# A hybrid recurrent layer step: the samples' state passes in one row, the residual's norm tile by tile in the second feed-forward product, and a third buffer of split weights from the merges on

## The chip, the cores and the metric

The kernel runs on one core of a Trainium2 chip. The metric is the time of one execution on the device in microseconds (us), the median of several runs. Engines go by short names: PE is TensorE, which multiplies matrices (PEld is its weight load), DVE is VectorE, ACT is ScalarE, POOL is GpSimd, and SP is SyncE, from whose queue most transfers are issued.

## What is computed

One inference step of a decoder layer, for a prompt of 512 tokens and for 8 samples of 4 tokens each, which share all weights. The width is 1024, the feed-forward width 4096. Cut to what matters:

```
proj = x @ w_in + b_in
h_gla = head_rmsnorm(gated_linear_scan(q, k, v, g, s_gla)) * silu(gr)     # GLA, 4 heads, dv 96
h_ml  = head_layernorm(mlstm_scan(q, k, v, i, f, c, n, m)) * sigmoid(mo)  # mLSTM
h_hg  = head_rmsnorm(gated_linear_scan(qh, kh, vh, log_f, s_hg)) * silu(hgt)  # HGRN2, 4 heads, dv 64
gates = sigmoid(mg)
merged = gates[0] * (h_gla @ w_up_gla) + gates[1] * (h_ml @ w_up_ml) + gates[2] * (h_hg @ w_up_hg)
x = layernorm(alpha * x + merged @ w_out, ln1_g, ln1_b)
hid = square(relu(x @ w_ff_up))
x = layernorm(alpha * x + hid @ w_ff_down, ln2_g, ln2_b)
```

In a gated linear scan each token's state is S_t = diag(exp g_t) S_{t-1} + k_t^T v_t, its output q_t S_t. The prompt starts from zero states, each sample from its own, and all final states are outputs too.

## The kernel before

**Layout and products.** The prompt's 512 columns and the samples' 32 stand side by side: T = 544 columns, worked on as two halves of 272 (HT). Activations lie with features on the 128 partitions. A product is computed on float32r operands of which each is split into a high part and the rest (names ending in h and l), as three products: high x high, high x low, low x high. `wload` (L133) does this for 1024 or fewer weight columns: a transfer from SP's queue into `raw` (three buffers), a copy by ScalarE into `wh` (L141), and VectorE's `raw - wh` into `wl` (L142). `wh` and `wl` have two buffers each, those of the pool `wp`. `mm` (L145) issues the matmuls, all on line L158: for each of the weights' 128-row blocks 3 x 2 matmuls of 272 columns. `gemm` (L163) is a load with its product, into one of two PSUM tiles named `g`, so that one is evacuated while the other is filled. `xgemm` (L172) is such a product with the layer's input `xh`, `xl`.

**Stages, in the order of the program.** First projections; the mLSTM; GLA's projections; GLA's scan by `gated` (L351); the merge of the mLSTM branch; HGRN2's projections; HGRN2's scan by `gated` again; the merge of the GLA branch; that of the HGRN2 branch; the output product with the first layer norm (`ln_tile`, `ln_end`); the feed-forward part in two blocks of 2048; the second layer norm, whose last products are shared with it.

**The scan.** `gated` takes the prompt in two units of 256 columns and the samples as a third. `levels` (L357) builds a unit's attention, level by level: a decay by VectorE and ScalarE, products with it on VectorE (`ke`, `qe`), four matmuls on TensorE (`lv`, L410) and a masked copy out. `chunk` (L461) then applies it and carries the state on. `sample` (L494) reads the samples' old states: for each of the two head pairs p the states come by a transfer on ScalarE's queue into `Ss`, and eight matmuls, one for each sample n, multiply `Ss` with that sample's queries `qx` (L509). Such a matmul has few columns, and the program writes it as one with two blocks of four; on the chip it is two matmuls. I call it a pass. Its weights have 96 columns in GLA and 64 in HGRN2, where those of other matmuls have 128. After a pair's passes the update of its states follows: `kvs` (L517) on TensorE, and a multiply and add on VectorE. `finish_rows` (L282) transposes normalised outputs (`oT`, L286) and multiplies them into the branch's gate.

**Merges.** `Merge` (L851) has three kinds of steps: `gates` (a product of 48 matmuls with the input, evacuated and put through a sigmoid), `split` (the branch's output into `hh`, `hl`), and `products` (the branch's product of 12 or 18 matmuls, multiplied by its gate and added to `merged`). The first two merges do four gates and then four products, twice over. The last one (`mr_`, L945) alternates: gate m + 1, product m.

**The residual.** After the output product `x1` (the memory of `merged`) holds the centred sum that the first layer norm takes. The feed-forward product uses a form of it that isn't normalised, and puts the norm in behind it (L1037 to L1039, with `ne` the negative mean and `rstd` the inverse deviation). The normalised `x1` itself is only wanted as the residual, in the second feed-forward product of the first block (L1062). Its three steps, an add of `ne` (L1052), a multiplication by `rstd` (L1054) and ScalarE's scale and bias (L1055), stand in the loop of the 16 tiles of the first feed-forward product of block 0: an add behind each even tile, the other two behind each odd one.

**What sets the order.** A scheduler puts the program's instructions in order for each engine by priority, which is at first the order in which they are written. `tc.high_priority(OFF)` puts a step as early as its operands allow; a negative argument puts it later. The passes have such a one, of 380 and 4 more for each sample:

```
with tc.high_priority(-(BEHIND + 4 * n)):
    nc.tensor.matmul(
        oT[0:dv, p * 64:(p + 1) * 64].rearrange("p (a b) -> p a b", a=2)[:, :, 4 * n:4 * n + 4],
        Ss[:, n, 0:dv], qx[:, p, n], start=False, stop=(p == 1 and n == 7))
```

Each engine then runs its queue in that order, and waits by semaphores for the others.

Of the kernel before, what the change touches and what calls it, by code (L numbers as in the profile page):

```python
# [6 lines left out]
F32 = mybir.dt.float32  # L7
F32R = mybir.dt.float32r
BF16 = mybir.dt.bfloat16
I32 = mybir.dt.int32  # L10
AF = mybir.ActivationFunctionType
ALU = mybir.AluOpType
PSUM = bass.MemoryType.PSUM

T = 544
# [6 lines left out]
ALPHA = 2.0 ** 0.25  # L22
# [2 lines left out]
NEG = -1e30  # L25
XMIN = -44.0
OFF = 1000000
BEHIND = 380
NF = 4
NWARM = 10  # L30
ADDP, MULP, AFFD = (), (), ()
# [4 lines left out]
V_L1G, V_L1B, V_L2G, V_L2B, V_QS, NV = 76, 84, 92, 100, 108, 109  # L36
# [7 lines left out]
def build(tc, I, O):  # L44
    nc = tc.nc
    with ExitStack() as ctx:
        const = ctx.enter_context(tc.tile_pool(name="const", bufs=1))
        wp = ctx.enter_context(tc.tile_pool(name="wp", bufs=2))
# [20 lines left out]
        for k in range(KD):  # L69
# [11 lines left out]
            for i, n in (sorted(terms) if k == KD - 1 else terms):  # L81
                w, a = ((fh, xh), (fl, xh), (fh, xl))[n]
                for hf in range(2):
                    nc.tensor.matmul(first_ps[i][hf], w[:, i * 128:(i + 1) * 128], a[:, k, hf * HT:(hf + 1) * HT],  # L84
                                     start=(k == 0 and n == 0), stop=(k == KD - 1 and n == 2))
# [43 lines left out]
        def vcol(c):  # L129
            return vec[:, c:c + 1]  # L130


        def wload(src, nk):  # L133

            n = nk * 128
            raw = wp.tile([128, 1024], F32, tag="raw", name="raw", bufs=3)
            nc.sync.dma_start(out=raw[:, 0:n], in_=src)
            h = wp.tile([128, 1024], F32R, tag="wh", name="wh")
            l = wp.tile([128, 1024], F32R, tag="wl", name="wl")
            with tc.high_priority(OFF):  # L140
                nc.scalar.activation(out=h[:, 0:n], in_=raw[:, 0:n], func=AF.Copy)  # L141
                nc.vector.tensor_tensor(out=l[:, 0:n], in0=raw[:, 0:n], in1=h[:, 0:n].bitcast(F32), op=ALU.subtract)  # L142
            return h, l
# [19 lines left out]
        def gemm(srcs, ah, al, ext=0):  # L163
            units = []
            for src, n in srcs:
                h, l = wload(src, n)
                units.append((h, l, n))
            ps = psg.tile([128, 2, 512], F32, tag="g", name="g")
            mm(ps, units, ah, al, ext)
            return ps if ext else ps[:, :, 0:HT]  # L170
# [4 lines left out]
        def halves(ap):  # L175
            return ap.rearrange("p (a b) -> p a b", a=2)
# [5 lines left out]
        def pool(name, bufs=1, side=None):  # L182
            st = ExitStack()
            return st, st.enter_context(tc.tile_pool(name=name, bufs=bufs, side=side, reuse_waits="tile"))
# [166 lines left out]
        def gated(q, k, b, sc, dv, vtok, sname, nt, gate):  # L351
# [142 lines left out]
            def sample():  # L494
                at, P, qx, k3 = (st[2][n] for n in ("at", "P", "qx", "k3"))
                oT = psr.tile([128, 512], F32, tag="r", name="oTs")
                for h in range(4):
                    nc.tensor.matmul(oT[0:dv, h * 32:(h + 1) * 32], vtok[0:32, 4, h * dv:(h + 1) * dv], at[0:32, h, 0:32],
                                     start=(h == 0), stop=False)
                v3 = stack_v(vtok[0:32, 4, 0:d4], d4)  # L500
                nb = 512 // dv // 4 * 4
                yield
                for p in range(2):
                    Ss = t1.tile([128, 8, 97], F32, tag="Ss", name="Ss")
                    nc.scalar.dma_start(out=Ss[:, :, 0:dv], in_=I[sname][p])
                    for n in range(8):

                        with tc.high_priority(-(BEHIND + 4 * n)):
                            nc.tensor.matmul(  # L509
                                oT[0:dv, p * 64:(p + 1) * 64].rearrange("p (a b) -> p a b", a=2)[:, :, 4 * n:4 * n + 4],  # L510
                                Ss[:, n, 0:dv], qx[:, p, n], start=False, stop=(p == 1 and n == 7))
                    yield
                    vxs = [spread_v(v3[:, (2 * p + e) * dv:(2 * p + e + 1) * dv], dv, True) for e in range(2)]
                    for n0 in range(0, 8, nb):
                        kvs = psr.tile([128, 512], F32, tag="r", name="kvs")
                        for e in range(2):
                            nc.tensor.matmul(kvs[:, 0:nb * dv], k3[:, p, e, :], vxs[e][:, n0 * dv:(n0 + nb) * dv], start=(e == 0), stop=(e == 1))  # L517
                        for n in range(n0, n0 + nb):
                            nc.vector.scalar_tensor_tensor(
                                Ss[:, n, 0:dv], Ss[:, n, 0:dv], P[:, p, 4 * n + 3:4 * n + 4],  # L520
                                kvs[:, (n - n0) * dv:(n - n0 + 1) * dv], ALU.mult, ALU.add)
                    nc.scalar.dma_start(out=O[sname + "_s"][p], in_=Ss[:, :, 0:dv])
                    yield
                oTs = t1.tile([97, 128], F32, tag="oTs", name="oTsb", bufs=1)
                nc.scalar.activation(out=oTs[0:dv], in_=oT[0:dv, 0:128], func=AF.Copy)
                o = psr.tile([128, 512], F32, tag="r", name="osm")
                for h in range(4):
                    nc.tensor.transpose(o[0:32, h * dv:(h + 1) * dv], oTs[0:dv, h * 32:(h + 1) * 32], ident[0:dv, 0:dv])
                on = rms_rows(32, o[0:32, 0:d4].rearrange("p (a b) -> p a b", a=4), dv)
                yield  # L530
                finish_rows(32, on, nt, gate, TP)
# [48 lines left out]
        for j in range(3):  # L580
            if M_X + j < NF:
                ps = first_ps[M_X + j]
            else:
                ps = xgemm(M_X + j)
                ps = [ps[:, 0, :], ps[:, 1, :]]
# [11 lines left out]
        for j in range(3):  # L597
            y = tile2([128, PADN], "cvy")
            ys.append(y)
            y = y[:, 0:NCV]  # L600
# [208 lines left out]

        pipe([ml_chunk(c) for c in (0, 4, 1, 2, 3)])  # L810
        mls.close()


        def open_kq():
# [22 lines left out]
        for j in range(2):  # L837
            ps = xgemm(M_K + j)
# [48 lines left out]
        hls, hlp = pool("hl")  # L887
        mgs, mgp = pool("mg")
        merged = mgp.tile([128, KD, T], F32, name="merged")
        mm_ = Merge(1, mgate, 3, "wup_ml", first=True)  # L890
        mm_.gates(0, gbp)
        mm_.split()
# [10 lines left out]
        for j in range(2):  # L903
# [5 lines left out]
            l = ftile("hl_")  # L909
# [118 lines left out]
        for blk in range(2):  # L1028
            hid = []
            deep = [hl3("hdh", "hh"), hl3("hdl", "hl")] + [w6.tile([128, 3 * T], F32R, tag="w6", name="hdw").rearrange("p (a b) -> p a b", a=3) for i in range(2)]  # L1030
            for m in range(16):
                ps = gemm([(I["wff1"][blk * 16 + m], KD)], lambda k: x1h[:, k, :], lambda k: x1l[:, k, :], ext=2)

                gw = fp.tile([128, 2], F32, tag="gw", name="gw", bufs=3)
                nc.scalar.activation(out=gw, in_=ps[:, 1, HT:HT + 2], func=AF.Copy)
                r_ = fp.tile([128, T], F32, tag="relu", name="relu", bufs=2)
                nc.vector.scalar_tensor_tensor(halves(r_), halves(ne), gw[:, 0:1], ps[:, :, 0:HT], ALU.mult, ALU.add)  # L1037
                nc.vector.tensor_tensor(out=r_, in0=r_, in1=rstd, op=ALU.mult)  # L1038
                nc.scalar.activation(out=r_, in_=r_, func=AF.Relu, bias=gw[:, 1:2])  # L1039
                nc.scalar.activation(out=r_, in_=r_, func=AF.Square)  # L1040
                if m < 6:
                    h, l = deep[m // 3][:, m % 3, :], deep[2 + m // 3][:, m % 3, :]
                else:
                    h = fp.tile([128, T], F32R, tag=f"hidh{m}", name="hidh")
                    l = fp.tile([128, T], F32R, tag=f"hidl{m}", name="hidl")
                split(h, l, r_)
                hid.append((h, l))
                if blk == 0:

                    y = x1[:, m // 2, :]  # L1050
                    if m % 2 == 0:
                        nc.vector.tensor_tensor(out=y, in0=y, in1=ne, op=ALU.add)  # L1052
                    else:
                        nc.vector.tensor_tensor(out=y, in0=y, in1=rstd, op=ALU.mult)  # L1054
                        nc.scalar.activation(out=y, in_=y, func=AF.Identity, scale=vcol(V_L1G + m // 2), bias=vcol(V_L1B + m // 2))  # L1055
            hh_, hl_ = (lambda k: hid[k][0]), (lambda k: hid[k][1])
            for m in range(KD if blk == 0 else KD - 2):
                w = I["wff2"][blk, m]
                ps = gemm([(w[:, 0:1024], 8), (w[:, 1024:2048], 8)], hh_, hl_)
                xm = halves(x1[:, m, :])  # L1060
                if blk == 0:
                    nc.vector.scalar_tensor_tensor(xm, xm, ALPHA, ps, ALU.mult, ALU.add)  # L1062
                else:
                    nc.vector.tensor_tensor(out=xm, in0=xm, in1=ps, op=ALU.add)
                    ln_tile(x1, m, slice(0, T), None)
# [49 lines left out]
        sts.close()  # L1115
        mgs.close()
        hls.close()
        gbs.close()


# [115 lines left out]
```

## Time and profile before

| | |
|---|---|
| Time, median of 3 runs | 937.22 us (937.22, 938.57, 936.66) |
| The profiled execution | 937.23 us, its span 935.1 us |
| TensorE's granted clock, mean | 0.995 |
| TensorE busy | 915.1 us, 98% |
| VectorE busy | 570.4 us, 61% |
| ScalarE busy | 436.9 us, 47% |
| GpSimd busy | 46.8 us, 5% |
| Bytes moved | 82.73 MB, mean 88 GB/s |

A row of the trace's timeline has the start in us from the span's start, the time from there to the end of the row's last instruction, engine, line, operation, what it writes and reads, the sizes and how many instructions the row joins; in brackets stand the idle time of the engine just before and what ended it. Matmuls are pipelined: the end of one is modelled and lies behind the start of the next, so times on TensorE are best taken from start to start. A row of the waits has the waiting engine and what it waited for, then the total in us, how many times, and the longest. The chain that ended last is followed back from the last instruction, at each step to what released it.

### The profile page before, as it was taken

Reading aid. Unit: us, or ns where it says so; the run is one execution under the profiler, and the core shown is the slowest. Engines: PE = TensorE matmul, PEld = TensorE weight load, DVE = VectorE, ACT = ScalarE, POOL = GpSimd, SP = SyncE. Lnnn points to the kernel's source line nnn. Section 1 sums busy time; section 2 is a strip of 40 time slices with the busy share of each in tenths; the row PEclk is TensorE's granted clock in tenths of the full one; section 3 lists DMA queues with packets and bytes.
Section 4 is the critical chain, followed back from the end, with each engine's and each line's share of the span. In section 5 each row is a group of like instructions: output and inputs, shape, how many; then the busy total and the mean of one; then the engine's idle time right before and its main releaser. Section 6 shows DMA issues by size and latency. Waiting matters only on the chain.

```text
span 935.1 us, 17425 instructions
## 1 busy us (share of the span) xinstructions
PE 915.1 (98%) x7271; PEld 897.1 (96%) x7271; DVE 570.4 (61%) x995; ACT 436.9 (47%) x822; POOL 46.8 (5%) x62
## 2 busy tenths in 40 slices
PE   9999999999999999999999989999999999999995
PEld 7998999999999989999999989999999999999994
DVE  5886468867877658785558695553222455545345
ACT  5395222975536755535444375542111355432215
POOL 1302130001001001000000000000000000000000
PEclk9999999999999999999999999999999999999998
DMA  7321232123122113023235222222222222322302
GB/s 265 122 71 66 72 114 73 37 82 100 63 93 94 54 29 119 27 79 107 68 118 149 99 71 88 91 91 90 91 86 79 86 91 91 91 90 81 100 23 96
DMA packets 37598, 82.73 MB, mean 88 GB/s; under 512 B 12708, under 2 KB 18340, under 8 KB 37520
## 3 DMA queue, kind: packets, MB, share of 16 engines
q1 hardware_dynamic: 25072, 73.28, 24.1%
q10 hardware_dynamic: 12384, 8.33, 3.1%
q8 instruction: 57, 0.93, 0.4%
q14 instruction: 21, 0.17, 0.1%
q0 software_dynamic: 64, 0.02, 0.0%
HBM read 76.51 MB, written 5.09 MB: 87 GB/s over the span
## 4 chain that ended last, share of the span: by engine, by line
PE 93%; DVE 4%; ACT 2%; DMA 1%; issue 1%; ACTq 0%; DVEq 0%
PE g L158 79%; PE lv L410 3%; PE g L84 3%; DVE wl L142 1%; PE o L467 1%; PE qkp L682 1%; PE oTs L509 1%; ACT wh L141 1%; PE oTm L770 1%; DVE merged L1054 1%; PE oT L286 0%; PE vt L259 0%; PE o L470 0%; DMA fw<-in_wfirst 0%; DVE merged L1052 0%
## 5 line engine op out<-in xcount | busy, mean ns | idle before, releaser
L141 ACT ACTIVATE wh<-raw 128x1024 fp32r<-128x1024 f32 (+2 forms) x139 | 133.3, 959 | 231.9 <-PE g L158 199.4
L142 DVE TENSOR_TENSOR wl<-raw,wh 128x1024 fp32r<-128x1024 f32 (+2 forms) x139 | 155.2, 1117 | 134.9 <-ACT wh L141 133.1
L158 PE MATMUL g<-xh,wl 128*128 128x272 f32 x752 | 161.9, 293 | 1.2 <-DVE wl L142 1.2
L158 PE MATMUL g<-xh,wh 128*128 128x272 f32 x752 | 161.0, 293 | 0.3 <-DVE z L833 0.3
L158 PE MATMUL g<-xl,wh 128*128 128x272 f32 x752 | 160.8, 292 | 0.0
L158 PEld LDWEIGHTS g<-xh,wl 128*128 128x128 f32 x752 | 119.4, 189 | 2.9 <-DVE wl L142 2.5
L158 PEld LDWEIGHTS g<-xh,wh 128*128 128x128 f32 x752 | 119.6, 189 | 1.5 <-DVE z L833 0.5
L158 PEld LDWEIGHTS g<-xl,wh 128*128 128x128 f32 x752 | 119.4, 189 | 1.0 <-issue 0.5
L158 PE MATMUL g<-x1h,wh 128*128 128x272 f32 (+1 forms) x512 | 106.5, 289 | 2.8 <-DVE relu L1037 2.8
L158 PE MATMUL g<-x1l,wh 128*128 128x272 f32 (+1 forms) x512 | 106.5, 289 | 0.0
L158 PE MATMUL g<-x1h,wl 128*128 128x272 f32 (+1 forms) x512 | 106.3, 289 | 0.0
L158 PEld LDWEIGHTS g<-x1h,wh 128*128 128x128 f32 x512 | 80.9, 189 | 3.3 <-DVE relu L1037 3.2
L158 PEld LDWEIGHTS g<-x1l,wh 128*128 128x128 f32 x512 | 81.2, 189 | 0.1
L158 PEld LDWEIGHTS g<-x1h,wl 128*128 128x128 f32 x512 | 80.9, 189 | 0.0
L1039 ACT ACTIVATE relu<-relu,gw 128x544 f32<-128x544 f32 x32 | 24.0, 750 | 73.8 <-DVE relu L1038 73.8
L158 PE MATMUL g<-hidh,wh 128*128 128x272 f32 x280 | 58.1, 288 | 0.0
L158 PE MATMUL g<-hidl,wh 128*128 128x272 f32 x280 | 58.1, 289 | 0.0
L158 PE MATMUL g<-hidh,wl 128*128 128x272 f32 x280 | 57.9, 288 | 0.0
L158 PEld LDWEIGHTS g<-hidh,wl 128*128 128x128 f32 x280 | 43.9, 188 | 0.1
L158 PEld LDWEIGHTS g<-hidl,wh 128*128 128x128 f32 x280 | 43.9, 188 | 0.0
L158 PEld LDWEIGHTS g<-hidh,wh 128*128 128x128 f32 x280 | 43.8, 188 | 0.0
L215 DVE TENSOR_SCALAR gb<-g,vec 128x544 f32<-128x544 f32 x24 | 18.8, 783 | 31.5 <-PE g L158 31.3
(398 smaller groups left out, 1661.0 us busy)
## 6 DMA issues: line engine op xcount, KB each, us to landing
raw<-in_wff SPq DMA_DIRECT2D x64, 512.0 KB, 3.5
raw<-in_win SPq DMA_DIRECT2D x47, 512.0 KB, 3.2
xr<-in_xT SPq DMA_DIRECT2D x16, 272.0 KB, 3.4
raw<-in_wout SPq DMA_DIRECT2D x8, 512.0 KB, 3.7
out_yT<-merged SPq DMA_DIRECT2D x8, 272.0 KB, 2.2
fw<-in_wfirst ACTq DMA_DIRECT2D x8, 256.0 KB, 5.4
raw<-in_wup_ml SPq DMA_DIRECT2D x8, 192.0 KB, 2.3
raw<-in_wup_gla SPq DMA_DIRECT2D x8, 192.0 KB, 2.3
```

What stands on the lines that cost most here:

```text
L84: nc.tensor.matmul(first_ps[i][hf], w[:, i * 128:(i + 1) * 128], a[:, k, hf * HT:(hf + 1) * HT], start=(k == 0 and n == 0), stop=(k == KD ...
L141: nc.scalar.activation(out=h[:, 0:n], in_=raw[:, 0:n], func=AF.Copy)
L142: nc.vector.tensor_tensor(out=l[:, 0:n], in0=raw[:, 0:n], in1=h[:, 0:n].bitcast(F32), op=ALU.subtract)
L158: nc.tensor.matmul(ps[:, hf, 0:w_], w, a(k)[:, hf * HT:hf * HT + w_], start=(k == 0 and s == 0), stop=(k == nk - 1 and s == 2))
L215: nc.vector.tensor_scalar(out, ps, vcol(col), XMIN, ALU.add, ALU.max)
L410: nc.tensor.matmul(lv[0:R, o:o + 2 * H].rearrange("p (a b) -> p a b", a=2), Kv[:, p, c * R:(c + 1) * R], Q[:, p, :, c * H:(c + 1) * H], st ...
L467: nc.tensor.matmul(o[:, h * dv:(h + 1) * dv], at[:, c * 4 + h, :], vtok[:, cc, h * dv:(h + 1) * dv], start=(h == 0), stop=(cc == 0 and h = ...
L509: nc.tensor.matmul(oT[0:dv, p * 64:(p + 1) * 64].rearrange("p (a b) -> p a b", a=2)[:, :, 4 * n:4 * n + 4], Ss[:, n, 0:dv], qx[:, p, n], s ...
L682: nc.tensor.matmul(ps[0:96, hf, 0:HT], w[:, i, h, :], a[h][:, hf * HT:(hf + 1) * HT], start=(n == 0), stop=(n == 2))
L770: nc.tensor.matmul(oT[0:97, h * 32 + 4 * n:h * 32 + 4 * n + 4], Cs[:, n, :], qF[h][:, 4 * n:4 * n + 4], start=False, stop=(h == 3 and n == 7))
L1039: nc.scalar.activation(out=r_, in_=r_, func=AF.Relu, bias=gw[:, 1:2])
L1054: nc.vector.tensor_tensor(out=y, in0=y, in1=rstd, op=ALU.mult)
```

## The change

**Passes.** The negative priority around L509 is gone, with its constant. The passes have the priority of the place where they are written.

**Residual.** The three steps are taken out of the loop of the first feed-forward product. In the loop of the second one, in block 0, they are written ahead of each tile's product, for that tile alone, and write a new tile `xn` (one buffer). `x1` keeps the centred sum until the evacuation, which now reads `xn`.

**Buffers.** A new pool `w3` is opened after the mLSTM's memory is closed, with one `wh` and one `wl` (8 KB of each partition). From the first merge on, every third call of `wload` takes its two tiles from it, and the others from `wp` as before.

```diff
--- before.py
+++ after.py
...
-BEHIND = 380
...
+        more_w, nload = [], [0]
+
         def wload(src, nk):
...
-            h = wp.tile([128, 1024], F32R, tag="wh", name="wh")
-            l = wp.tile([128, 1024], F32R, tag="wl", name="wl")
+            w_ = more_w[0] if more_w and nload[0] % 3 == 2 else wp
+            nload[0] += 1
+            h = w_.tile([128, 1024], F32R, tag="wh", name="wh")
+            l = w_.tile([128, 1024], F32R, tag="wl", name="wl")
...
                     for n in range(8):
-
-                        with tc.high_priority(-(BEHIND + 4 * n)):
-                            nc.tensor.matmul(
-                                oT[0:dv, p * 64:(p + 1) * 64].rearrange("p (a b) -> p a b", a=2)[:, :, 4 * n:4 * n + 4],
-                                Ss[:, n, 0:dv], qx[:, p, n], start=False, stop=(p == 1 and n == 7))
+                        nc.tensor.matmul(
+                            oT[0:dv, p * 64:(p + 1) * 64].rearrange("p (a b) -> p a b", a=2)[:, :, 4 * n:4 * n + 4],
+                            Ss[:, n, 0:dv], qx[:, p, n], start=False, stop=(p == 1 and n == 7))
...
         mls.close()
+        w3s, w3p = pool("w3")
...
         merged = mgp.tile([128, KD, T], F32, name="merged")
+        more_w.append(w3p)
         mm_ = Merge(1, mgate, 3, "wup_ml", first=True)
...
                 hid.append((h, l))
-                if blk == 0:
-
-                    y = x1[:, m // 2, :]
-                    if m % 2 == 0:
-                        nc.vector.tensor_tensor(out=y, in0=y, in1=ne, op=ALU.add)
-                    else:
-                        nc.vector.tensor_tensor(out=y, in0=y, in1=rstd, op=ALU.mult)
-                        nc.scalar.activation(out=y, in_=y, func=AF.Identity, scale=vcol(V_L1G + m // 2), bias=vcol(V_L1B + m // 2))
             hh_, hl_ = (lambda k: hid[k][0]), (lambda k: hid[k][1])
             for m in range(KD if blk == 0 else KD - 2):
                 w = I["wff2"][blk, m]
+                if blk == 0:
+
+                    xn = fp.tile([128, T], F32, tag="xn", name="xn", bufs=1)
+                    nc.vector.tensor_tensor(out=xn, in0=x1[:, m, :], in1=ne, op=ALU.add)
+                    nc.vector.tensor_tensor(out=xn, in0=xn, in1=rstd, op=ALU.mult)
+                    nc.scalar.activation(out=xn, in_=xn, func=AF.Identity, scale=vcol(V_L1G + m), bias=vcol(V_L1B + m))
...
                 if blk == 0:
-                    nc.vector.scalar_tensor_tensor(xm, xm, ALPHA, ps, ALU.mult, ALU.add)
+                    nc.vector.scalar_tensor_tensor(xm, halves(xn), ALPHA, ps, ALU.mult, ALU.add)
...
         hls.close()
+        w3s.close()
```

Three places show what the scheduler makes of it. A row has the line, the operation, what it writes and reads, the size and how many such instructions follow one another; the line numbers of after are 3 to 6 higher. The first place is TensorE in the HGRN2 samples: `oTs` from `qx` and `Ss` is a pass, `lv` a level of the prompt's first unit, `kvs` the states' update, `g` from `xh` or `xl` a gate product of the merge that follows. Before:

```order
L410 MATMUL lv<-qe_3863,ke_3861 128x128 x4
L509 MATMUL oTs<-qx,Ss 64x2x4 x2
L410 MATMUL lv<-qe_3862,ke_3860 128x128 x4
L158 MATMUL g<-xh,wl 128x272 x2
L509 MATMUL oTs<-qx,Ss 64x2x4
L158 MATMUL g<-xh,wh 128x272 x2
L158 MATMUL g<-xl,wh 128x272 x2
L509 MATMUL oTs<-qx,Ss 64x2x4
L158 MATMUL g<-xh,wl 128x272 x2
L517 MATMUL kvs<-vx,k_3915 128x512
L158 MATMUL g<-xh,wh 128x272 x2
L509 MATMUL oTs<-qx,Ss 64x2x4
```

And after:

```order
L413 MATMUL lv<-qe_3866,ke_3864 128x128 x4
L510 MATMUL oTs<-qx,Ss 64x2x4 x8
L413 MATMUL lv<-qe_3865,ke_3863 128x128 x4
L510 MATMUL oTs<-qx,Ss 64x2x4 x2
L518 MATMUL kvs<-vx,k_3918 128x512
L510 MATMUL oTs<-qx,Ss 64x2x4 x6
L161 MATMUL g<-xh,wl 128x272 x2
```

Before, the 16 passes stand in 15 rows among the products, one of them of two passes; after, in rows of 8, 2 and 6, and the products follow. In GLA the 16 passes stood in one row of nine and seven lone ones, and stand in rows of 11 and 5.

The second place is VectorE where the first feed-forward product begins: `rstd<-m,rstd` belongs to the end of the first layer norm, `wl` is a weight split, `relu<-ne,gw,g` is the evacuation of a tile. Before:

```order
L996 TENSOR_TENSOR rstd<-m_6319,rstd 128x272
L1052 TENSOR_TENSOR merged<-merged,ne 128x544 x8
L142 TENSOR_TENSOR wl<-raw,wh 128x1024
L1037 SCALAR_TENSOR_TENSOR relu<-ne,gw,g 128x544
L1054 TENSOR_TENSOR merged<-merged,rstd 128x544 x8
L142 TENSOR_TENSOR wl<-raw,wh 128x1024
L1037 SCALAR_TENSOR_TENSOR relu<-ne,gw,g 128x544
```

And after:

```order
L1000 TENSOR_TENSOR rstd<-m_6322,rstd 128x272
L1058 TENSOR_TENSOR xn<-merged,ne 128x544
L145 TENSOR_TENSOR wl<-raw,wh 128x1024
L1041 SCALAR_TENSOR_TENSOR relu<-ne,gw,g 128x544
L1059 TENSOR_TENSOR xn<-xn,rstd 128x544
L1042 TENSOR_TENSOR relu<-relu,rstd 128x544
L145 TENSOR_TENSOR wl<-raw,wh 128x1024
L1041 SCALAR_TENSOR_TENSOR relu<-ne,gw,g 128x544
```

Eight adds and eight multiplications stood in rows there; one of each is left, and the other seven stand in the second feed-forward product, one ahead of each product's evacuation.

The third place is TensorE where the last merge begins: `oT` are the last transposes of the HGRN2 scan, whose outputs are multiplied by the gate and split into `hh` and `hl`, and `g` from `hh` is the first product with them. Before:

```order
L286 MATMUL oT<-ident,on 128x128 x2
L158 MATMUL g<-xl,wh 128x272
L158 MATMUL g<-xh,wl 128x272 x2
L158 MATMUL g<-xh,wh 128x272 x2
L158 MATMUL g<-xl,wh 128x272 x2
L158 MATMUL g<-xh,wl 128x272 x2
L158 MATMUL g<-xh,wh 128x272 x2
L158 MATMUL g<-xl,wh 128x272 x2
L158 MATMUL g<-xh,wl 128x272 x2
L158 MATMUL g<-hh,wh 128x272 x2
```

And after:

```order
L289 MATMUL oT<-ident,on 128x128 x2
L161 MATMUL g<-xh,wh 128x272
L161 MATMUL g<-xl,wh 128x272 x2
L161 MATMUL g<-xh,wl 128x272 x2
L161 MATMUL g<-hh,wh 128x272 x2
```

15 products stood between the two, and five do now. Another place of the same kind lies behind the GLA samples: between the last level of the prompt's first unit (`lv` from `kg`) and the level before it stood 73 products, and stand 95 now.

More of the change, by code (lines that the diff above doesn't have):

```diff
@@ L811, in build @@
         mls.close()
+        w3s, w3p = pool("w3")
+        pass
         def open_kq():
```

## The prediction

> **What bounds the kernel now.** I read the page's first part and the chain that ended last, then the waits, then the timeline at the places that both name. From the page:
>
> ```profile
> span 935.1 us, 17425 instructions
> ## 1 busy us (share of the span) xinstructions
> PE 915.1 (98%) x7271; PEld 897.1 (96%) x7271; DVE 570.4 (61%) x995; ACT 436.9 (47%) x822; POOL 46.8 (5%) x62
> ```
>
> And the longest piece of the chain (start, us, what):
>
> ```profile
> 551.50 288.96 PE g L158 x2293
> ```
>
> TensorE is busy 98% of the span, and for 289 us on end the chain is nothing but products: 2293 in 288.96 us, 0.126 us each, with no wait between. Something can be won only where matmuls start further apart than that. TensorE's waits name such places (us in total, times, longest):
>
> ```profile
> PE g L158 <- DVE relu L1037: 2.8, 2, 2.2
> PE g L158 <- DVE wl L142: 1.9, 7, 0.7
> ...
> PE lv L410 <- DVE qe L402: 0.7, 1, 0.7
> ```
>
> The wait for relu lies ahead of the first feed-forward product, that for wl in the last merge, that for qe behind the GLA samples: the change touches all three. An idle time counts from where a matmul's end is modelled, which is later than the next start could have been. So I measure a gap from start to start: next start, minus start of the last pair, minus two matmuls (0.25 us).
>
> **The residual's norm.** VectorE at the start of the first feed-forward product:
>
> ```profile
> 537.53 5.17 DVE L1052 TENSOR_TENSOR merged<-merged,ne 128x544 f32<-128x544 f32 x8 [0.16 <-ACT ne L997]
> 542.62 1.22 DVE L142 TENSOR_TENSOR wl<-raw,wh 128x1024 fp32r<-128x1024 f32 x1
> 543.76 0.78 DVE L1037 SCALAR_TENSOR_TENSOR relu<-ne,gw,g 128x544 f32<-128x544 f32 x1
> 544.45 5.17 DVE L1054 TENSOR_TENSOR merged<-merged,rstd 128x544 f32<-128x544 f32 x8
> ```
>
> TensorE at the same time, around the two gaps:
>
> ```profile
> 541.94 0.41 PE L158 MATMUL g<-x1h,wl 128*128 128x272 f32 x2
> 544.59 0.53 PE L158 MATMUL g<-x1h,wh 128*128 128x272 f32 x2 [2.24 <-DVE relu L1037]
> ...
> 550.51 0.41 PE L158 MATMUL g<-x1h,wl 128*128 128x272 f32 x2
> 551.50 0.52 PE L158 MATMUL g<-x1h,wh 128*128 128x272 f32 x2 [0.57 <-DVE relu L1037]
> ```
>
> Eight adds stand ahead of the first evacuation (L1037), eight multiplications ahead of the second, 5.17 us each, while both PSUM tiles of the products are full. TensorE stands for 544.59 - 541.94 - 0.25 = 2.40 us and for 551.50 - 550.51 - 0.25 = 0.74 us, 3.1 us together. With the change one add (5.17 / 8 = 0.65) is left ahead of the first and one multiplication ahead of the second. From 537.53 the queue is 0.65 + 1.22 + 0.78, so the first tile is free at about 540.2 (541 if the split wl must wait a little for wh), and TensorE asks for it at 542.19: at least 1 us to spare. **Term: -3.1 us**; by the row of waits it is -2.8, and 0 if the evacuation is late for another reason.
>
> The other seven tiles' steps go to the second feed-forward product. There VectorE waits for each product's end (first row), and the affine step that ScalarE has to do took 5.97 / 8 = 0.75 us (second row):
>
> ```profile
> DVE merged L1062 <- PE g L158: 31.5, 8, 4.0
> ...
> 545.20 5.97 ACT L1055 ACTIVATE merged<-merged,vec 128x544 f32<-128x544 f32 x8 [1.95 <-DVE merged L1054]
> ```
>
> A product there is 96 matmuls, 12.1 us, and in each VectorE idles 31.5 / 8 = 3.9 us before the evacuation. Into that fit the 0.65 + 0.65 us that it gets more, and 0.75 us on ScalarE. L1064 now waits for the affine step too; behind it in VectorE's queue stand the next tile's add and a split, and TensorE waits for neither within a product, since the other PSUM tile takes 12.1 us to fill. **Term: 0.** Without both covers it would be 7 x (0.65 + 0.65 + 0.75) = 14.4 us.
>
> **The third buffer.** In the last merge a gate product (48 matmuls) and a branch product (12) alternate. TensorE in one such turn and at the first output product:
>
> ```profile
> 461.62 0.41 PE L158 MATMUL g<-xl,wh 128*128 128x272 f32 x2
> 462.20 0.52 PE L158 MATMUL g<-xh,wl 128*128 128x272 f32 x2 [0.16 <-DVE wl L142]
> ...
> 479.05 0.41 PE L158 MATMUL g<-ml,wh 128*128 128x272 f32 x2
> 480.17 0.52 PE L158 MATMUL g<-mh,wl 128*128 128x272 f32 x2 [0.71 <-DVE wl L142]
> ```
>
> The two halves of the split that this turn waits for, on ScalarE and on VectorE:
>
> ```profile
> 459.82 1.06 ACT L141 ACTIVATE wh<-raw 128x1024 fp32r<-128x1024 f32 x1 [3.35 <-PE g L158]
> ...
> 460.92 1.23 DVE L142 TENSOR_TENSOR wl<-raw,wh 128x1024 fp32r<-128x1024 f32 x1
> ```
>
> The split of the next gate's weights takes 1.06 + 1.23 = 2.3 us and starts only when the gate before it has released its buffer; the 12 matmuls of the branch and the first four of the gate, 16 x 0.126 = 2.0 us, do not cover it. The gap is 462.20 - 461.62 - 0.25 = 0.33 us, at the output product 0.87 us. The row of waits counts seven; with the other five like the first that is 6 x 0.33 + 0.87 = 2.85 us. With three buffers a gate's weights go where the branch product before the last gate had its own, and that is free a whole gate, 6 us, earlier. **Term: -2.9 us**, from -1.9 (the idle time as the row of waits has it) to -3.4, since TensorE's idle time ahead of all products in the seven turns came to that:
>
> ```profile
> PEld g L158: 3.4, 7
> ```
>
> That row is the weight loads' idle time (us, times), which begins when the load before has ended. VectorE at 61% and ScalarE at 47% of the span have room for splits that come earlier. The feed-forward products, in the chain's long piece, wait for no split now, and gain nothing.
>
> **The passes.** In the HGRN2 samples a pass (L509) is two matmuls with 64 weight columns among products with 128. TensorE there:
>
> ```profile
> 328.16 0.40 PE L509 MATMUL oTs<-qx,Ss 128*64 128x8 f32 x4
> 328.49 1.16 PE L410 MATMUL lv<-qe,ke 128*128 128x128 f32 x8
> ...
> 330.05 0.52 PE L158 MATMUL g<-xh,wh 128*128 128x272 f32 x2
> 330.40 0.41 PE L158 MATMUL g<-xl,wh 128*128 128x272 f32 x2
> 330.74 0.28 PE L509 MATMUL oTs<-qx,Ss 128*64 128x8 f32 x2
> 330.95 0.52 PE L158 MATMUL g<-xh,wl 128*128 128x272 f32 x2
> ```
>
> From 330.05 to 330.95 run four products (0.50) and one pass: a lone pass costs 0.40 us. From its first start to the next instruction's, a lone pass takes 330.95 - 330.74 = 0.21 us and a row of two 328.49 - 328.16 = 0.33: the second one added 0.12. So each pass that joins a row saves 0.28 us. The order had 15 rows for these 16 passes and has three now (8, 2 and 6): 12 x 0.28 = 3.4 us. In the GLA samples, with 96 columns, two lone passes four products apart:
>
> ```profile
> 185.60 0.26 PE L509 MATMUL oTs<-qx,Ss 128*96 128x8 f32 x2
> ...
> 186.30 0.26 PE L509 MATMUL oTs<-qx,Ss 128*96 128x8 f32 x2
> ```
>
> One costs 186.30 - 185.60 - 0.50 = 0.20 us. Seven lone ones join a row; if one in a row is as cheap as the 0.12 above, that is 7 x 0.08 = 0.6 us, if it is no cheaper 0; I take 0.3. **Term: -3.7 us**, from -4.0 to 0 (should a pass cost 0.40 us wherever it stands).
>
> [...]
>
> **What the new order moves.** Behind the GLA samples TensorE waited 0.7 us for a level's operand (the row of waits). Between the level before it and that level now stand 95 products instead of 73, 22 x 0.126 = 2.8 us more: **-0.7 us** (from -0.7 to 0). At the last merge it is the other way: between the last transposes and the first product with hh stand 5 products instead of 15, 1.3 us less cover for the multiplication by the gate and hh's split. And the saved 3.7 us let levels, kvs and transposes of both sample parts come sooner against VectorE and ScalarE. Of such waits the trace of before had the one of 0.7 us; I add one of 0.7 in the HGRN2 samples and half of one, 0.4, at the hh product: **+1.1 us** in all, between 0 and 4. The stops of the queues change little: SP's loads of the last merges trade places by one, the states' loads on ScalarE's queue keep theirs well ahead of the passes.
>
> **Sum.** -3.1 + 0 - 2.9 - 3.7 - 0.7 + 1.1 = -9.3 us. The profiled execution took 937.23 us (its span of 935.1 and 2.1 around it), within 0.01 of the median of the runs, 937.22. 937.2 - 9.3 = 927.9 us.
>
> **Rivals.** (1) In the sample parts the level chains of VectorE and ScalarE become the bound, so that passes and level wait give nothing and the new waits stay. For it: few products are left between some levels. Against it: of 935 us TensorE had one such wait. 937.2 - 3.1 - 2.9 + 1.1 = 932.3. (2) The third buffer does nothing, as its splits wait for something else, a load say. Against it: ScalarE had idled 3.35 us ahead of the split, and a product ended that, not a load. 927.9 + 2.9 = 930.8. [...] (4) Slower: the norm's steps come to lie between the products of the second feed-forward stage, because the affine step stands behind a split in ScalarE's queue and that split waits until the running product releases a buffer. It decides once wait and chain together outlast the 12.1 us that the other PSUM tile gives; then add, split, multiplication and affine step, 0.65 + 1.22 + 0.65 + 0.75 = 3.3 us, stand between products seven times, 23 us: 951 us. Against it: 3.9 us of idle time per product, and 3.3 is far from 12.1.
>
> **Numbers.** Chances: forecast 0.82, (1) 0.09, (2) 0.04, (3) 0.02, (4) 0.03. The range: every gain at its end and no new wait, -3.1 - 3.4 - 4.0 - 0.7 = -11.2, gives 926.0; gains of 2.8 + 1.9 + 3.4 with new waits of 3 give -5.1, 932.1, and with it most of (1) and all of (2). So 925.8 to 932.3. A measurement of this kernel tells about 0.2% (1.9 us) from no change. Faster 0.95, same 0.02, slower 0.03.
>
> **What would show it.** Right: no wait for relu at the first feed-forward product, none of TensorE for wl in the last merge, three rows of 64-column passes there at 0.12 us a pass, and no more than some 2 us of waits that were not there. Wrong: waits of TensorE for lv, kvs or hh of several us, splits still behind the running product, a row of eight passes that takes 8 x 0.40 us, or products of the second feed-forward stage that start late.

## The result, and the profile after

The changed kernel takes 931.36 us (median of 4 runs, 930.18 to 932.45), the kernel before, beside it, 937.84 us. The ratio is 0.9932, with an interval from 0.9912 to 0.9952: 6.4 us less, between 4.5 and 8.2. Forecast were 9.3 us less, 927.9 us, and a range from 925.8 to 932.3: the time lies in the range, 0.9 us below its upper end.

The page of after, span and engines, the two lines that were shown of before:

```profile
span 928.3 us, 17440 instructions
...
PE 910.1 (98%) x7271; PEld 896.1 (97%) x7271; DVE 566.6 (61%) x995; ACT 436.8 (47%) x822; POOL 48.5 (5%) x62
```

The same work in a span that is 6.8 us shorter. The longest piece of the chain, in the feed-forward part (start, us, what):

```profile
533.16 300.57 PE g L161 x2385
```

It was 288.96 us long with 2293 matmuls and began behind the second wait for relu; now it begins ahead of where these waits were. TensorE's waits in after (us in total, times, longest):

```profile
PE g L161 <- ACT W L430: 1.5, 1, 1.5
...
PE lv L413 <- DVE qe L405: 0.9, 1, 0.9
PE g L161 <- ACT hh L182: 0.8, 1, 0.8
...
PE g L161 <- DVE merged L883: 0.2, 1, 0.2
```

The waits for relu (2.8 us) and for wl (1.9 us) are gone, as forecast. So is that of 0.7 us for qe, at the last level of the prompt's first unit; the row for qe above belongs to another level, at 258.30. But five waits of more than 0.35 us stand in the trace that were not there before: from start to start 1.63 us at 211.45, 1.05 at 258.30, 0.37 at 248.07, 0.39 at 260.31 and 0.96 at 426.47, 4.4 us together, where 1.1 had been allowed.

VectorE at the first feed-forward product of after, where eight adds and eight multiplications stood:

```profile
533.87 0.72 DVE L1058 TENSOR_TENSOR xn<-merged,ne 128x544 f32<-128x544 f32 x1 [0.16 <-ACT ne L1001]
534.81 1.23 DVE L145 TENSOR_TENSOR wl<-raw,wh 128x1024 fp32r<-128x1024 f32 x1 [0.22 <-ACT wh L144]
535.96 0.77 DVE L1041 SCALAR_TENSOR_TENSOR relu<-ne,gw,g 128x544 f32<-128x544 f32 x1
536.65 0.72 DVE L1059 TENSOR_TENSOR xn<-xn,rstd 128x544 f32<-128x544 f32 x1
```

The first tile is evacuated at 535.96 + 0.77 = 536.7, 2.9 us behind the add's start; worked out were 2.65, or some 3.5 with a wait of wl for wh. In the second product VectorE still idles ahead of each evacuation as it did (31.5 us in eight waits before):

```profile
DVE merged L1064 <- PE g L161: 31.7, 8, 4.0
```

There is one thing in the trace of after that no step of the prediction had. TensorE around the HGRN2 samples' passes, in stretches (start to end, length, busy time of PE, PEld, DVE, ACT and POOL with counts, then the granted clock, DMA share and GB/s):

```profile
329.00:332.76 3.76, 3.76 (x43) 3.32 (x42) 3.51 (x9) 1.52 (x6) 0.00 (x0) 1.00 0.18 57
332.76:336.18 3.42, 3.42 (x16) 3.42 (x17) 0.38 (x2) 1.42 (x7) 0.00 (x0) 0.50 0.00 0
336.18:340.00 3.82, 3.82 (x32) 3.78 (x32) 3.22 (x10) 1.28 (x6) 0.00 (x0) 1.00 0.00 0
```

For 3.42 us behind the rows of passes the granted clock is 0.50. TensorE is busy all the time by the trace, but gets 16 matmuls done where 32 pass in the next 3.82 us. A matmul of a product then starts 0.227 us after the one before it, instead of 0.126. The sum over these matmuls, of what each took above its usual distance, is 1.6 us. Before had one such stretch, in the mLSTM (119.72 to 123.14); after has that one too (110.90 to 114.31), and the second here.

The rows themselves went as forecast. TensorE in after:

```profile
329.01 1.10 PE L510 MATMUL oTs<-qx,Ss 128*64 128x8 f32 x16
330.04 1.16 PE L413 MATMUL lv<-qe,ke 128*128 128x128 f32 x8
331.13 0.40 PE L510 MATMUL oTs<-qx,Ss 128*64 128x8 f32 x4
```

Eight passes take 330.04 - 329.01 = 1.03 us, 0.13 each; lone they cost 0.40.

### The profile page after: what moved, and what is told of

Same layout as the page of the kernel before. It is cut to its first block, busy times and chain, and to the rows that moved or that the text cites. A ratio compares the mean times of both kernels' runs of the same rounds, so it can differ in the third digit from the quotient of the medians.

```text
span 928.3 us, 17440 instructions
## 1 busy us (share of the span) xinstructions
PE 910.1 (98%) x7271; PEld 896.1 (97%) x7271; DVE 566.6 (61%) x995; ACT 436.8 (47%) x822; POOL 48.5 (5%) x62
## 4 chain that ended last, share of the span: by engine, by line
PE 94%; DVE 3%; ACT 1%; issue 1%; DMA 0%; ACTq 0%; DVEq 0%
PE g L161 81%; PE g L83 3%; PE lv L413 3%; PE o L470 1%; PE qkp L683 1%; PE oTm L771 1%; PE oTs L510 1%; PE vt L262 0%; PE oT L289 0%; DMA fw<-in_wfirst 0%; PE o L473 0%; PE kvp L478 0%; PE m L990 0%; ACT merged L1113 0%; PE dps L372 0%
## 5 line engine op out<-in xcount | busy, mean ns | idle before, releaser
L417 DVE COPY_PREDICATED at<-lmask,lv 128x512 f32<-128x512 int32 (+1 forms) x32 | 26.2, 818 | 24.7 <-PE lv L413 24.3
```

The costliest lines, as they stand in the source:

```text
L417: nc.vector.copy_predicated(atv.rearrange("p h (n m) -> p h n m", m=2 * m)[:, :, :, m:2 * m], lmask[0:R, li, 0:H].rearrange("p (n m) -> p ...
```

## The experiments

All differences are to the kernel before, timed beside them (medians 936.85, 936.83 and 937.63 us in the three groups of runs). To see where the time sits, the trace is cut at the starts of five matmuls: GLA is from the first level `lv` from `kg` to the first from `kh`; HG from the HGRN2 samples' first `oTs` from `at` to the first output product; "out" from there to the first feed-forward product, FF1 from there to the second one, FF2 from there to the last matmul. In us, with the stretches of half clock that the trace has in a stage in brackets (between GLA and HG lie 10.4 us in all of them; where the third buffer is in use from the first merge on, GLA holds 11 matmuls less, 1.4 us):

| kernel | GLA | HG | out | FF1 | FF2 |
|---|---|---|---|---|---|
| before | 141.95 | 152.30 | 49.47 | 102.11 | 293.36 |
| after | 142.50 | 148.72 (1) | 48.53 | 98.79 | 293.51 |
| e1_residual | 141.94 | 152.30 | 49.46 | 98.57 | 293.18 |
| e2_buffer | 143.96 (1) | 150.93 | 48.53 | 103.00 (1) | 293.30 |
| e3_passes | 142.58 (1) | 148.72 | 49.46 | 102.86 (1) | 293.22 |
| e4_no_passes | 147.16 (3) | 150.92 | 48.53 | 98.79 | 293.51 |
| e5_buffer_last | 142.56 (1) | 146.92 | 48.54 | 98.79 | 293.51 |
| e6_buffer_last_turn | 142.55 (1) | 146.17 | 48.55 | 98.83 | 293.56 |
| e7_rows_apart | 141.77 | 146.74 | 48.53 | 98.80 | 293.51 |
| e8_filled_wait | 141.93 | 152.33 | 49.46 | 101.93 | 293.22 |
| e9_apart_and_turn | 141.77 | 146.02 | 48.55 | 98.83 | 293.56 |
| e10_changed_again | 142.50 | 148.66 (1) | 48.53 | 98.79 | 293.51 |

**Each part alone.** My theory after the result, called W below (not the tile of that name), is that the new waits in GLA belong to the third buffer. The rival, P, is that they belong to the passes' edit, to which the prediction had put all new waits down. First the residual alone, the kernel before with:

```diff
-                if blk == 0:
-                    y = x1[:, m // 2, :]
...
+                if blk == 0:
+                    xn = fp.tile([128, T], F32, tag="xn", name="xn", bufs=1)
...
-                    nc.vector.scalar_tensor_tensor(xm, xm, ALPHA, ps, ALU.mult, ALU.add)
+                    nc.vector.scalar_tensor_tensor(xm, halves(xn), ALPHA, ps, ALU.mult, ALU.add)
```

> The residual's norm alone. TensorE's order is that of before. If the term of the prediction is right: 3.1 us less than before (934.7 beside 937.8), no wait for relu at the first feed-forward product, no gap over 0.2 us in the second. If the seven tiles' steps cost something in the second product, up to 14.4 us, the gain is smaller and gaps stand there.

Measured: 934.05 us, ratio 0.9959 (0.9945 to 0.9973), 3.8 us less, between 2.5 and 5.2. No gap over 0.21 us in either feed-forward product, and FF2 is as long as before.

The third buffer alone:

```diff
...
-            h = wp.tile([128, 1024], F32R, tag="wh", name="wh")
-            l = wp.tile([128, 1024], F32R, tag="wl", name="wl")
+            w_ = more_w[0] if more_w and nload[0] % 3 == 2 else wp
+            nload[0] += 1
+            h = w_.tile([128, 1024], F32R, tag="wh", name="wh")
+            l = w_.tile([128, 1024], F32R, tag="wl", name="wl")
...
+        more_w.append(w3p)
         mm_ = Merge(1, mgate, 3, "wup_ml", first=True)
```

> The third buffer alone. Theory now (W): the new waits of the changed kernel in GLA (1.6 us of a gate product for its PSUM tile at 211 us, 1.05 us of a level for qe at 258 us, two of 0.4 us) come from this edit, which brings the products of the mLSTM merge forward against the levels; then the six waits for wl (2.8 us) and the wait of 0.9 us for the last level of unit 0 go, these come, and the kernel is within 1 us of before. Rival (P): they come from the passes' edit; then this kernel is 2.9 to 3.7 us faster than before and has none of them. No stretch of half clock behind the HGRN2 samples by either.

Measured: 937.18 us, ratio 1.0002 (0.9989 to 1.0014): 0.2 us more, between 1.0 less and 1.3 more. TensorE's waits in this kernel:

```profile
PE g L162 <- DVE relu L1043: 2.2, 1, 2.2
PE g L162 <- ACT hh L183: 1.9, 1, 1.9
PE g L162 <- ACT W L431: 1.5, 1, 1.5
...
PE lv L414 <- DVE qe L406: 0.9, 1, 0.9
```

The waits of after are here, with no change to the passes, and no row for wl is left: W holds and P falls. The buffer does what it was said to do in the last merge, and pays it back elsewhere. The wait for hh is twice that of after: here no product is left between the last transposes and the first product with hh, where after has five. What I had not expected is a stretch of half clock at 189.69, and one behind the wait for relu (544.68).

The passes alone:

```diff
-                        with tc.high_priority(-(BEHIND + 4 * n)):
-                            nc.tensor.matmul(
...
+                        nc.tensor.matmul(
```

> The passes in rows alone, GLA's 16 in one row, HGRN2's in rows of 8, 2 and 6. The rows should save 3.4 us and 0.2 us. By W, what comes against it is a stretch of 3.4 us at half clock behind the HGRN2 rows, which costs 1.6 us, and the wait for hh of about 1 us: 1 to 2 us faster than before. By P the GLA waits of 3.4 us come too: 1 to 2 us slower than before. If the half clock there was chance and doesn't belong to the rows, the granted clock behind them is 1.0.

Measured: 933.67 us, ratio 0.9957 (0.9940 to 0.9974), 4.0 us less, between 2.4 and 5.6. That is more than either theory gave, and its interval leaves out P's sign. HG is 152.30 - 148.72 = 3.58 us shorter. No half clock stands behind the HGRN2 rows in this profile, but one does in GLA (187.85).

The changed kernel without the passes' edit:

```diff
+BEHIND = 380
...
+                        with tc.high_priority(-(BEHIND + 4 * n)):
+                            nc.tensor.matmul(
...
-                        nc.tensor.matmul(
```

> The changed kernel with the passes' negative priority put back; TensorE's order is that of the changed kernel as far as the HGRN2 samples. By W: the GLA waits stay, the half clock behind the HGRN2 samples goes (1.6 us less) and the lone passes cost 3.4 us again: about 1 to 2 us slower than the changed kernel. By P: the GLA waits of 3.4 us go too: 1 to 2 us faster than the changed kernel.

Measured: 935.03 us, ratio 0.9979 (0.9968 to 0.9991), 2.0 us less than before where the changed kernel has 6.4. The GLA waits stay (1.63 us at 215.17, 1.06 at 261.99), as W said; the loss against the changed kernel, 4.4 us by the ratios, is more than W's 1 to 2. In the profile there are three stretches of half clock on end in GLA, 187.10 to 197.34. They make up that profile's 4.7 us more in GLA; whether its other runs have them isn't shown (their mean granted clock goes from 0.989 to 0.994).

**The buffer where its waits were.** The changed kernel with the buffer in use from the last merge on:

```diff
-        more_w.append(w3p)
         mm_ = Merge(1, mgate, 3, "wup_ml", first=True)
...
+        more_w.append(w3p)
         mr_ = Merge(2, hgate, 2, "wup_hg", fin=(mh, ml))
```

> The changed kernel with the third buffer in use only from the last merge on, where the waits for wl were. If its gain of 2.8 us there is real and is only taken back by the waits that it brings in GLA, this kernel has neither the seven waits for wl nor those in GLA (1.6, 1.05, 0.4 and 0.4 us): 3.8 + 4.0 + 2.8 less a wait for hh of 1 to 2 us, since only 5 products lie ahead of it, so 8.6 to 9.6 us faster than before and 2 to 3 us faster than the changed kernel. If the buffer's gain is an illusion, its time is the sum of the two other edits, 7.8 us faster than before or less.

Measured: 928.82 us, ratio 0.9903 (0.9890 to 0.9916), 9.1 us less, between 7.9 and 10.3. Of TensorE's waits these two are left for wl and hh:

```profile
PE g L161 <- ACT hh L182: 0.8, 1, 0.8
...
PE g L161 <- DVE wl L145: 0.5, 1, 0.5
```

The one for wl lies at 69 us, far ahead of this merge. GLA's waits are gone too, but for two small ones (0.29 and 0.45) that the passes alone had as well; the one for hh, 0.97 us from start to start, stays. The buffer's gain was real.

The other turn of the loads, in that kernel:

```diff
-            w_ = more_w[0] if more_w and nload[0] % 3 == 2 else wp
+            w_ = more_w[0] if more_w and nload[0] % 3 == 0 else wp
```

> As the kernel with the buffer from the last merge on, but with the other turn of the three loads in the third buffer; by the order 25 products lie between the last transposes and the first product with hh instead of 5. If the wait for hh is a matter of that cover, it is gone here (25 x 0.126 = 3.2 us against some 2.7 us of chain): 1 to 2 us faster than the kernel with 5. If it is set by something else (a queue on VectorE), it stays.

Measured: 927.14 us, ratio 0.9894 (0.9881 to 0.9907), 9.9 us less. The wait for hh is gone from the trace and one of 0.39 us for wl has come; HG is 0.75 us shorter. The medians are 1.7 us apart, but the intervals overlap.

**The half clock.** The rows apart, in the kernel with the buffer in the last merge:

```diff
-                        nc.tensor.matmul(
+                        with tc.high_priority(-400 * p):
+                            nc.tensor.matmul(
```

> As the kernel with the buffer from the last merge on, but the second pair's passes are put 400 later: the HGRN2 passes stand in two rows of 8, with 41 rows of other work between them, and GLA's second eight in rows of 1, 1, 3 and 3 among products. If low activity of TensorE over a stretch of 3.4 us is what brings a stretch of half clock, it is rarer here behind both sample parts and the mean granted clock rises by about 0.002 (one stretch), the time falls by up to 1.6 us. If the half clock has nothing to do with the rows, clock and time stay.

Measured: 926.70 us, ratio 0.9886 (0.9873 to 0.9899), 10.7 us less. The mean granted clock was 0.994 in all four runs, where the five of the kernel with the rows together had 0.990 to 0.993. Stretches of TensorE at GLA's passes, with the rows together (the kernel with the buffer in the last merge):

```profile
184.86:188.27 3.41, 3.41 (x37) 3.41 (x37) 2.92 (x5) 3.36 (x11) 0.21 (x1) 1.00 0.00 0
188.27:191.68 3.41, 3.41 (x17) 3.41 (x16) 2.42 (x6) 3.41 (x10) 0.00 (x0) 0.50 0.21 62
```

And apart, the same times:

```profile
184.86:188.27 3.41, 3.41 (x32) 3.41 (x32) 2.50 (x4) 3.36 (x9) 0.00 (x0) 1.00 0.03 2
188.27:191.68 3.41, 3.41 (x33) 3.40 (x32) 2.50 (x6) 3.07 (x11) 0.20 (x1) 1.00 0.19 61
```

17 matmuls at clock 0.50 with the passes together, 33 at 1.00 with products between them. TensorE is busy throughout in both by the trace. The clock's part is plain; the time's is less so. The medians are 2.1 us apart (928.82 and 926.70), but the intervals overlap, and GLA is 0.79 us shorter and not the 1.5 of a stretch: a new wait of 0.95 us, at 210.5, is part of the reason.

Products in the idle time of the kernel before (they add work whose result isn't used):

```diff
+                if blk == 0 and m == 2:
+                    fill = psr.tile([128, 512], F32, tag="r", name="fill")
+                    for i in range(18):
+                        nc.tensor.matmul(fill[:, 0:HT], x1h[:, 0, 0:128], x1h[:, 0, 0:HT], start=True, stop=True)
                 ps = gemm([(I["wff1"][blk * 16 + m], KD)], lambda k: x1h[:, k, :], lambda k: x1l[:, k, :], ext=2)
```

> The kernel before, with 18 more matmuls of 272 columns put where TensorE waits 2.40 us for relu; they write a PSUM tile that nobody reads, and take 18 x 0.126 = 2.3 us. The wait that the residual's steps cause stays as long as it was. If the idle time of 2.4 us is what brings the stretch of half clock that other runs show right behind it (at 541 to 548 us), no run has it, the mean granted clock rises from 0.992 to 0.994 and the time falls by 1 to 1.6 us. If it comes from elsewhere, clock and time are those of before, or up to 0.3 us more.

Measured: 937.20 us, ratio 0.9997 (0.9987 to 1.0006): 0.3 us less, between 1.2 less and 0.6 more. The clock did as expected: 11 of 12 runs have 0.993 to 0.997, while before has 0.992 in 15 of the 17 runs beside them. In this kernel and in the one with the third buffer alone, behind the wait:

```profile
543.50:547.00 3.50, 3.50 (x30) 3.50 (x29) 3.50 (x7) 3.46 (x5) 0.00 (x0) 1.00 0.35 131
```

```profile
544.68:548.09 3.41, 3.41 (x18) 3.41 (x17) 3.41 (x6) 3.41 (x6) 0.00 (x0) 0.50 0.32 129
```

The time didn't follow. FF1 says why in part: with the half clock it takes 102.9 to 103.0 us, without 101.9 to 102.1, a price of 0.9 us and not 1.6, since the second wait for relu (0.74 us) vanishes when the product ahead of it is slow. The rest stays open.

**Together.** Rows apart with the other turn:

```diff
-            w_ = more_w[0] if more_w and nload[0] % 3 == 2 else wp
+            w_ = more_w[0] if more_w and nload[0] % 3 == 0 else wp
...
+                        with tc.high_priority(-400 * p):
```

> The two that helped together: rows apart, and the other turn of the third buffer, which puts 25 products ahead of the first product with hh. If their gains are of different kinds (half clock behind GLA's passes, 1 to 1.6 us; wait for hh, 0.97 us), they add: 10.5 to 12 us faster than before, about 1 us faster than the rows apart alone, mean granted clock 0.994. If the wait for hh is only replaced by another, it is as fast as the rows apart alone.

Measured: 926.76 us, ratio 0.9886 (0.9872 to 0.9899). By its trace it is the shortest of all: HG is 0.72 us shorter than with the rows apart alone, and the wait for hh is gone. The medians don't show it (926.76 and 926.70, in different groups). So the gain of the turn stays unproved, and either kernel is 10.7 us faster than before.

The changed kernel again, as it is:

> The changed kernel once more, on the same chip as the run beside it. Its order has GLA's passes in rows of 11 and 5. If such rows bring a stretch of half clock in most executions, the profile is likely to show one at some 187 to 197 us (five of the six profiles of kernels with at least 11 in a row have it, none of the four with at most 9), and the mean granted clock is 0.990 to 0.992. The time should be 6.4 us less than before, between 4.5 and 8.2.

Measured: 930.19 us, ratio 0.9930 (0.9916 to 0.9944), 6.6 us less. The half clock stands behind the HGRN2 rows again (332.24 to 335.65) and not in GLA: the place was wrong.

## Why the prediction was right, and where it was not

**The residual, -3.1.** Right. FF1 is 3.3 us shorter in after, and alone the edit gave 3.8 (2.5 to 5.2). What it may give beyond the two waits is the stretch of half clock behind the longer one, 0.9 us where an execution has it (two of the three profiles in which TensorE is idle there for 2.4 us).

**The seven other tiles, 0.** Right: FF2 takes 293.36 us before, 293.51 after, and 293.18 with this edit alone.

**The passes, -3.7.** Right in size: HG is 3.58 us shorter where nothing but the rows changed, forecast 3.4. In GLA a pass in the row of 11 took 1.82 / 11 = 0.165 us against 0.20 alone, which for seven is some 0.2 us, forecast 0.3. A lone pass was not free: in before it cost 0.40 us in the HGRN2 samples, in the row of eight in after it takes 0.13, and the rows alone gave 4.0 us (2.4 to 5.6). What failed is that nothing was held against the rows. Of the profiles of kernels whose GLA passes stand in a row of 11 or more, all seven have at least one stretch of half clock in the two sample parts, and of the five others none. One costs 1.5 us in GLA (143.96 against 142.50 in the same order) and 1.6 us in HG.

**The third buffer, -2.9.** The size was right for the place I priced and the term was wrong for the edit. I priced the last merge. But the buffer is in use from the first merge on, and the order there changes as well: the merge's products come forward against GLA's levels. Alone, the edit gives nothing (+0.2). VectorE in after at the longest of the new waits:

```profile
210.05 0.54 DVE L303 TENSOR_TENSOR on<-osm,ss 32x384 f32<-32x384 f32 x1
210.52 0.40 DVE L400 TENSOR_TENSOR E<-bg 128x256 f32<-128x256 f32 x1
210.85 0.67 DVE L428 TENSOR_TENSOR W<-bg 128x512 f32<-128x512 f32 x1
211.45 0.97 DVE L520 SCALAR_TENSOR_TENSOR Ss<-Ss,P,kvs 128x96 f32<-128x96 f32 x4
212.35 0.71 DVE L883 TENSOR_TENSOR merged<-g,gb 128x544 f32<-128x544 f32 x1
```

And TensorE:

```profile
213.21 0.49 PE L161 MATMUL g<-xh,wh 128*128 128x272 f32 x2 [1.47 <-ACT W L430]
```

The row names ScalarE's W, which ends at 213.1 too, but a gate product doesn't read W. What it can't start without is a PSUM tile, and the tile's evacuation (L883) ends at 212.35 + 0.71 = 213.06, behind four steps of the samples and of the next level in VectorE's queue. A trace bears this out: in the kernel with the rows apart and the other turn, a product of the same merge waits 0.94 us behind the same steps, and there the row names the evacuation itself:

```profile
209.43 0.70 DVE L884 TENSOR_TENSOR merged<-g,gb 128x544 f32<-128x544 f32 x1
...
210.28 0.49 PE L161 MATMUL g<-hh,wh 128*128 128x272 f32 x2 [0.78 <-DVE merged L884]
```

The reading is still from rows alone; no run here took one of those steps away.

**The level's wait, -0.7, and the new waits, +1.1.** The wait of 0.9 us for the last level of unit 0 went as forecast, and this one of 1.63 us came in at the same place. The term of +1.1 is the step that failed: I put new waits down to the passes, in HGRN2 and at the last merge, and took two small ones. They came to 4.4 us, and all five come with the buffer: the kernel with the passes alone has none above 0.45. Four lie in GLA, for which the sum held no new wait at all. The one for hh lay where I had looked, and was 0.96 us instead of 0.4; it hangs on the products ahead of it: 2.0 us with none (the buffer alone), 0.96 with five, gone with 25.

**The sum.** -3.3 (FF1), -0.9 (out), -3.6 (HG), +0.6 (GLA), +0.2 (FF2) and +0.3 (all ahead of GLA's levels) make the -6.8 us between the two profiled executions. Against -9.3 that lacks 2.5 us: new waits of 4.4 instead of 1.1, 3.3 more, and a stretch of half clock, 1.6, less some 2.4 us that no term of the sum holds. Some 1.1 us of these, between the two profiled executions, are chance and not the change: TensorE's first 1270 matmuls are the same in both kernels, and the last of them starts at 165.52 us before and at 164.44 after, while over all twelve profiles, with the same matmuls, it starts between 163.49 and 166.35. (The +0.3 is this -1.1 and the 1.4 us of the 11 matmuls that moved there from GLA.) The other 1.3 are smaller gains that I haven't put down one by one. So the terms that failed cost 4.9 us, and that the time still came out inside the range is in part luck. Of the rivals, none came true as it was told. Rival 1 has the right kind of event, levels that become late, with the wrong cause; rival 2 has the right time for the buffer, nothing, with the wrong reason; rival 4 fell.

## What to carry to other kernels

A buffer that removes a wait in one stage changes the order in every stage in which it is in use. Price it there too, or switch it on only where the wait is: that alone was worth 2.7 us by the ratios here (6.4 and 9.1, with intervals that just overlap). Where TensorE is the bound, look at a stretch's granted clock too, and not only at its waits: behind the rows of small matmuls in after TensorE is busy all the time by the trace, and yet 3.42 us at clock 0.50 cost 1.6 us there. In the two kernels here whose passes were put in rows apart, with products between them, no stretch of half clock stands in the sample parts (in the first of them the clock is 1.00 at GLA's passes, 184.86 to 191.68).

## What the runs showed of the hardware

Between 30 and 905 us of the profiles, stretches of half clock (granted clock 0.50) are 3.41 us long, as in after at 110.90 to 114.31 and 332.76 to 336.18, or 10.24 us, as in the changed kernel without the passes' edit at 187.10 to 197.34. With the third buffer alone, one stands behind a wait of 2.4 us (544.68 to 548.09). Before has a wait of 2.40 us at the same place, and its clock is 1.00 behind it. With matmuls put into that wait it is 1.00 too (543.50 to 547.00). In after, one stands behind rows of passes in which the profile shows TensorE busy in every slice (3.76 of 3.76 us). So the profile's busy time alone doesn't tell where such a stretch follows.

Nor does the order of the instructions tell it. Of four profiles with the same order in GLA, two have a half clock there (the changed kernel without the passes' edit, the buffer alone) and two have none (after, twice). What brings such a stretch about was not shown by these runs.
